# Seven block products in place of eight for the second MLP products of two chunks, with the sums of weight blocks made by accumulating DMAs

## The chip, the cores and the metric

The kernel runs on one core of a Trainium2 chip. The metric is the device time of one execution in microseconds. Three runs of the kernel before took 1099.1, 1102.78 and 1100.49 us; the median is 1100.49 us. The profile shows one further execution whose span, from the first to the last instruction, is 1099.7 us.

## The reference

One layer of a hybrid decoder for 512 prompt tokens and 32 new tokens (8 sequences of 4), which share all weights. Cut to the part that matters here:

```python
    y_m = h.astype(x.dtype) @ w_m_out                       # h: mLSTM output, gated
    merged = jax.nn.sigmoid(gc) * y_conv + jax.nn.sigmoid(gm) * y_m
    x1 = layer_norm(ALPHA * x + merged @ w_o, ln1_g, ln1_b)
    hid = jnp.square(jax.nn.relu(x1 @ w_ff1))               # 1024 -> 4096
    x2 = layer_norm(ALPHA * x1 + hid @ w_ff2, ln2_g, ln2_b) # 4096 -> 1024
```

Ahead of that stand the input projections (`w_in`), a short causal convolution of width 3 and the chunked mLSTM with its matrix states. Results are float32.

## The kernel before

**Layout.** All 544 tokens are held together, transposed: 8 tiles of 128 features (partitions) by 544 tokens, in large buffers called `slot0` to `slot7`. A half is 272 tokens; one half of one product fills part of one PSUM bank.

**One weight tile.** A weight tile is 1024 x 128 values, 512 KB, loaded by SyncE into one of three buffers `wr` (`wload`, L105) and split into two fp32r parts: `wh` by a cast on ScalarE (L140), `wl`, the remainder, by a subtract on VectorE (L141); each has three buffers too. Activations are kept as such pairs as well. A product is then `wh` by the high part, `wh` by the low part and `wl` by the high part, over 8 blocks of 128 input features and 2 halves of tokens: 48 matmuls of 272 columns per weight tile, all at L151 (`mm`, called by `mtile`).

**Order of the work.** Input projections with the prompt's mLSTM between them; the decode mLSTM, whose 32 states are read, updated and written back (L496 to L511; the write `out_cs_dram<-cr` is issued by GpSimd); convolution; `w_conv_out`, the gates and `w_m_out`; `w_o` and the first norm, half of the tokens by half; then the MLP in four chunks of 1024 hidden features (`for ck in range(4)`). A chunk is eight first-product tiles, each followed by relu, square and split (`act1`, L783 to L786), and eight second-product tiles, each added to `x1` by VectorE (L810, for the first chunk L807). The last chunk's second products go half by half with the last norm beside them. The instructions of the engines are put in order at build time by a scheduler that follows the program's dependencies and the buffers' reuse; each engine then runs its own list strictly in order.

**What the change touches.** Tiles 120 to 127 are the second products of chunk 1 and tiles 136 to 143 those of chunk 2; tiles 128 and 132 are the first two hidden tiles that chunk 2 now takes ahead. GpSimd issues no DMA and runs no instruction between 740 and 1040 us, SyncE only the weight loads.

Of the kernel before, what the change touches and what calls it, by code (L numbers as in the profile page):

```python
# [12 lines left out]
PSUM = bass.MemoryType.PSUM  # L13

# [17 lines left out]
# columns of the packed small operands  # L32
# [10 lines left out]
# order of the weight tiles  # L43
W_K, W_Q, W_O, W_V, W_CONV, W_YC, W_GC, W_GM, W_OUT, W_FF = 0, 8, 16, 24, 32, 56, 64, 72, 88, 96


@with_exitstack
def tile_hybrid(ctx: ExitStack, tc: tile.TileContext, xT, wt, wg, pk, caug,
# [118 lines left out]
    mstk = ExitStack()          # what the mLSTM keeps to its end  # L167
# [12 lines left out]
    pstk = ExitStack()          # what only the prompt's mLSTM needs  # L180
# [69 lines left out]
    # rows that matmuls spread over the partitions, in exact halves: c, w_inter of the prompt  # L250
# [31 lines left out]
    # per-token columns: a, w_inter, ws, exp(-m)  # L282
# [14 lines left out]
    # decay weights of S, transposed (s on partitions)  # L297
# [17 lines left out]
    qT, so = slot(3), slot(4)  # L315
# [9 lines left out]
    for ft in range(KT):  # L325
        h, d0 = ft // 2, (ft % 2) * P
        ps = mtile(W_V + ft, xh, xl)
        vt = tmp.tile([P, NT], F32, name=f"vt{ft}", tag="cg")
# [5 lines left out]
        vr = tmp.tile([P, 4, NS], F32, name=f"vr{ft}", tag="vr")  # L334
# [118 lines left out]
    # P: rows hi, hi, lo, lo, against v's rows hi, lo, hi, lo  # L453
# [7 lines left out]
    # k*ws: rows hi, hi, lo, lo of the 32 tokens  # L461
# [13 lines left out]
    # q*w_inter, hi and lo, each batch's columns alone  # L475
# [38 lines left out]
    finish(dp, nsb, NS, NC, 512)  # L514
    dstk.close()
    mstk.close()

# [1 line left out]
    bc = slot(5)  # L519
# [3 lines left out]
    NU = 2 + SEQ + DB * 6  # L523
    for ft in range(KT):
        ps = mtile(W_CONV + 3 * ft, xh, xl)
        cg = tmp.tile([P, NT], F32, name=f"cg{ft}", tag="cg")
        nc.scalar.copy(hview(cg), pv(ps))
        ps = mtile(W_CONV + 3 * ft + 1, xh, xl)
        ue = tmp.tile([P, NU], F32, name=f"ue{ft}", tag="ue")
# [22 lines left out]
    nc.sync.dma_start(conv_o, uco)

    def split(src, dh, dl, ft):
        nc.scalar.copy(r(dh[:, ft]), src)
        nc.vector.tensor_tensor(r(dl[:, ft]), src, dh[:, ft], op=ALU.subtract)

    bh, bl = slot(2), slot(3)
    split_ahead(W_YC, W_YC + 1)
    for ft in range(KT):  # L560
        split(bc[:, ft], bh, bl, ft)
    y1 = slot(5)
# [3 lines left out]
    for ft in range(KT):  # L566
        ps = mtile(W_GC + ft, xh, xl)
        sg = tmp.tile([P, NT], F32, name=f"sgc{ft}", tag="cg")
# [4 lines left out]
    late = pool("late")  # L573
    hh, hl = slot(6, late), slot(7, late)
    for ft in range(KT):
        split(so[:, ft], hh, hl, ft)
    mh, ml = slot(2), slot(3)
    for ft in range(KT):
        ps = mtile(W_GM + 2 * ft, xh, xl)
        sg = tmp.tile([P, NT], F32, name=f"sgm{ft}", tag="cg")  # L580
# [4 lines left out]
        split(sg, mh, ml, ft)  # L585

# [4 lines left out]
    x1 = slot(0)  # L591
    nc.sync.dma_start(x1, xT)
# [4 lines left out]
    lnp = pool("lnp", 2)  # L597

    def resident(i0, places, eng=nc.vector):
        out = [wsplit(i0 + j, eng) for j in range(3)]  # L600
        spots = []
        for j in range(3, KT):
            if not spots:
                n, pl = places.pop(0)
                t = pl.tile([P, KT * NT], F32R, name=f"res{i0}_{n}", tag=f"slot{n}")
                spots = [(t[:, 2 * g * KT * P:(2 * g + 1) * KT * P],
                          t[:, (2 * g + 1) * KT * P:(2 * g + 2) * KT * P]) for g in range(2)]
            hi, lo = spots.pop(0)
# [4 lines left out]
        return out  # L613

    def half(i, ft, w, ah, al, cs, mid=None):
# [4 lines left out]
    def lt(nm, tag, bufs=2, n=HN):  # L620
        return lnp.tile([P, HW], F32, name=nm, tag=tag, bufs=bufs)[:, :n]

# [6 lines left out]
    def rstd(nm, src):  # L629
        n = src.shape[1]  # L630
        rs = lt(nm, "lnr", n=n)
        nc.scalar.activation(rs, src, AF.Ln, bias=epst)
        nc.scalar.activation(rs, rs, AF.Exp, scale=-0.5)
        t = lt(nm + "n", "lnn", 1, n)         # a Newton step: y * (1.5 - 0.5 * (var + eps) * y * y)
# [5 lines left out]
    xh1, xl1 = slot(1), slot(5)  # L640

    def norm1a(hf, s):
# [3 lines left out]
        q = lt(f"aq{hf}", "lnq")  # L646
        for j in range(4):
            nc.vector.tensor_tensor(pair(x1, j, cs), pair(x1, j, cs), b2(pmn[:, :HN]),
                                    op=ALU.subtract)
            sq = lnp.tile([P, 2, HN], F32, name=f"asq{hf}{j}", tag="lnsq")  # L650
            nc.scalar.activation(sq, pair(x1, j, cs), AF.Square)
            if j > 0:
                nc.vector.tensor_tensor(sq, sq, sq0, op=ALU.add)
            sq0 = sq
        nc.vector.tensor_tensor(q, sq[:, 0], sq[:, 1], op=ALU.add)
        return q

    def norm1b(hf, q):
# [3 lines left out]
        rs = rstd(f"ar{hf}", pvr[:, :HN])  # L662
# [12 lines left out]
    res = resident(W_OUT, [(4, slots), (6, late), (7, late)])  # L675
    later = {}      # pieces of a norm, by the tile of the next half after which they come
# [5 lines left out]
    for hf in range(2):  # L682
        s1 = lt(f"as{hf}", "lns")
# [23 lines left out]
    def norm2_part(hf, ft, ps, st):  # L707
        """x = acc + ps, less the mean c of the first four tiles; sums of it and its squares"""
# [21 lines left out]
        for f in todo:  # L730
# [3 lines left out]
            sq = lt(f"bsq{hf}{f}", "lnsq2", n=n)  # L734
# [10 lines left out]
    def norm2(hf, st):  # L745
# [5 lines left out]
        m2 = lt(f"bm2{hf}", "lnm", n=n)  # L751
        nc.scalar.activation(m2, pmn[:, :n], AF.Square)
        nc.vector.tensor_tensor(m2, pq[:, :n], m2, op=ALU.subtract)
        rs = rstd(f"br{hf}", m2)
        ms = lt(f"bms{hf}", "lnm", n=n)
# [21 lines left out]
    for ck in range(4):  # L777
        dh, dl = (slot(2), slot(3)) if ck % 2 == 0 else (slot(6, late), slot(7, late))

        def act1(ft, src, cs, view):  # L780
            rl = tmp.tile([P, NT], F32, name=f"rl{ck}_{ft}_{cs.start}", tag="cg")
            rl_ = rl[:, :cs.stop - cs.start]
            nc.scalar.activation(view(rl_), src, AF.Relu)  # L783
            nc.vector.tensor_tensor(rl_, rl_, rl_, op=ALU.mult)  # L784
            nc.scalar.copy(r(dh[:, ft, cs]), rl_)  # L785
            nc.vector.tensor_tensor(r(dl[:, ft, cs]), rl_, dh[:, ft, cs], op=ALU.subtract)  # L786

        i0 = W_FF + 16 * ck
        if ck == 0:
            res = resident(i0, [(4, slots), (6, late), (7, late)], nc.gpsimd)  # L790
            for hf in range(2):
                for ft in range(KT):
                    run(ft)
                    act1(ft, half(i0 + ft, ft, res[ft], xh1, xl1, hv[hf]), hv[hf], lambda t: t)
        else:
            for ft in range(KT):
                act1(ft, pv(mtile(i0 + ft, xh1, xl1)), slice(0, NT), hview)
        if ck == 0:
            products_psum(2)
        if ck == 3:  # L800
            products_psum(4)
        if ck < 3:
            for ft in range(KT):
                ps = mtile(i0 + 8 + ft, dh, dl)
                a_ = hview(x1[:, ft])
                if ck == 0:
# [121 lines left out]
```

## Time and profile before

| What | Value |
|---|---|
| runs, median | 1099.1, 1102.78, 1100.49; 1100.49 us |
| span of the profiled execution | 1099.7 us |
| mean granted TensorE clock in it | 0.988 |
| busy: PE, VectorE, ScalarE, GpSimd | 97%, 49%, 32%, 13% of the span |
| HBM read, written | 97.32 MB, 11.81 MB |

The profile gives no time around the span of its execution; the median of the three runs stands 0.8 us above that span. PE is TensorE's matmul, PEld its weight load, which runs beside it; DVE is VectorE, ACT ScalarE, POOL GpSimd, SP SyncE. Matmuls are pipelined, so the duration of one (some 0.29 us) is longer than the distance from one to the next.

### The profile page before, as it was taken

How to read it: one execution, taken by the hardware profiler on the slowest of the kernel's cores; microseconds unless marked ns; L12 is line 12 of the kernel's file. 1: busy time of each engine (PE TensorE's matmuls, PEld its weight loads, DVE VectorE, ACT ScalarE, POOL GpSimd, SP SyncE). 2: the span in 40 equal slices, each digit the busy share in tenths (PEclk: the TensorE clock that was granted, in tenths of full speed). 3: DMA queues.
4: the chain of work that ended last, by engine and by line, in shares of the span. 5: the costliest groups of instructions: out<-in, count | busy, mean ns of one | idle time of the engine just before them, and what ended most of it. 6: DMA issues, size and time to landing. Idle time of an engine off the chain costs nothing.

```text
span 1099.7 us, 19420 instructions
## 1 busy us (share of the span) xinstructions
PE 1071.2 (97%) x8351; PEld 1060.0 (96%) x8351; DVE 535.5 (49%) x882; ACT 347.9 (32%) x516; POOL 143.0 (13%) x161
## 2 busy tenths in 40 slices
PE   8999999999999989999999999899999999999994
PEld 8999999999999989999999999899999999999994
DVE  5533223365578778522143359742344234334576
ACT  6431222232234334213222225441233133123432
POOL 1000230000017563003200004200000000000033
PEclk9999999999999999999999999899999999999997
DMA  6222222211136775222222342112222222222201
GB/s 233 98 78 77 97 83 90 77 45 53 40 135 203 241 209 162 95 96 77 97 79 95 123 171 96 58 58 75 80 97 77 97 81 93 94 80 97 96 23 60
DMA packets 34349, 110.37 MB, mean 100 GB/s; under 512 B 3928, under 2 KB 6232, under 8 KB 34008
## 3 DMA queue, kind: packets, MB, share of 16 engines
q1 hardware_dynamic: 31704, 100.69, 28.2%
q0 software_dynamic: 2560, 8.46, 2.0%
q8 instruction: 65, 1.06, 0.4%
q14 instruction: 20, 0.16, 0.1%
HBM read 97.32 MB, written 11.81 MB: 99 GB/s over the span
## 4 chain that ended last, share of the span: by engine, by line
PE 90%; DVE 4%; DMA 3%; ACT 1%; issue 1%; POOL 0%; SPq 0%; DVEq 0%; POOLq 0%; ACTq 0%
PE ps L151 82%; DMA cr<-in_caug_dram 1%; DMA out_cs_dram<-cr 1%; PE u L419 1%; PE pq L496 1%; PE n L405 1%; DVE slot L733 1%; PE S L386 1%; PE n L402 1%; DMA wr<-in_wt_dram 1%; DVE bq L743 1%; DVE slot L671 0%; PE us L507 0%; PE ht L367 0%; PE kt L412 0%
## 5 line engine op out<-in xcount | busy, mean ns | idle before, releaser
L151 PE MATMUL ps<-slot,wh 128*128 128x272 f32 (+1 forms) x4640 | 801.2, 290 | 3.9 <-DVE slot L671 1.8
L151 PEld LDWEIGHTS ps<-slot,wh 128*128 128x128 f32 x4640 | 669.0, 189 | 7.0 <-DVE slot L671 2.5
L151 PE MATMUL ps<-slot,wl 128*128 128x272 f32 (+1 forms) x2320 | 498.2, 289 | 0.0
L151 PEld LDWEIGHTS ps<-slot,wl 128*128 128x128 f32 x2320 | 371.6, 189 | 0.7
L140 ACT CAST wh<-wr 128x1024 fp32r<-128x1024 f32 x145 | 152.1, 1050 | 501.1 <-PE ps L151 437.3
L141 DVE TENSOR_TENSOR wl<-wr,wh 128x1024 fp32r<-128x1024 f32 x142 | 174.1, 1226 | 205.8 <-ACT wh L140 201.7
L151 PE MATMUL ps<-slot,res 128*128 128x272 f32 (+2 forms) x720 | 92.8, 289 | 0.0
L151 PEld LDWEIGHTS ps<-slot,res 128*128 128x128 f32 x720 | 91.3, 188 | 0.3
L726 POOL TENSOR_TENSOR slot<-slot,bc 128x288 f32<-128x288 f32 (+1 forms) x6 | 5.8, 992 | 360.2 <-ACT bc L724 360.2
L810 DVE TENSOR_TENSOR slot<-ps,slot 128x544 f32<-128x544 f32 x16 | 11.6, 725 | 59.3 <-PE ps L151 59.3
L503 POOL TENSOR_SCALAR km<-kk,pkt 128x256 fp32r<-128x256 f32 x32 | 37.3, 1168 | 14.6 <-PE us L507 7.8
L492 ACT CAST ch<-cr 128x516 fp32r<-128x516 f32 x32 | 19.9, 623 | 49.6 <-DMA cr<-in_caug_dram 28.7
L785 ACT CAST slot<-rl 128x544 fp32r<-128x544 f32 (+1 forms) x40 | 22.2, 556 | 37.2 <-DVE rl L784 37.1
L786 DVE TENSOR_TENSOR slot<-rl,slot 128x544 fp32r<-128x544 f32 (+1 forms) x40 | 24.4, 611 | 19.6 <-ACT slot L785 19.4
L509 DVE SCALAR_TENSOR_TENSOR cr<-cr,dec,us 128x258 f32<-128x258 f32 x64 | 29.3, 475 | 3.3 <-PE us L507 3.1
L324 POOL TENSOR_SCALAR slot<-slot,pkt 128x544 f32<-128x544 f32 x8 | 16.8, 2096 | 107.9 <-ACT slot L323 107.9
L493 DVE TENSOR_TENSOR cl<-cr,ch 128x516 fp32r<-128x516 f32 x32 | 22.1, 697 | 17.6 <-ACT ch L492 17.5
L784 DVE TENSOR_TENSOR rl<-rl 128x544 f32<-128x544 f32 (+1 forms) x40 | 24.3, 607 | 11.8 <-ACT rl L783 11.8
L570 POOL TENSOR_TENSOR slot<-slot,sgc 128x544 f32<-128x544 f32 x8 | 14.5, 1809 | 88.1 <-ACT sgc L569 88.1
L783 ACT ACTIVATE rl<-ps 128x544 f32<-128x544 f32 (+1 forms) x40 | 21.2, 529 | 14.3 <-PE ps L151 14.3
L496 PE MATMUL pq<-ch,qm 128*64 128x258 f32 x64 | 18.3, 292 | 5.9 <-ACT wh L140 3.2
L141 POOL TENSOR_TENSOR wl<-wr,wh 128x1024 fp32r<-128x1024 f32 x3 | 7.3, 2423 | 124.9 <-PE am L645 121.2
(258 smaller groups left out, 715.2 us busy)
## 6 DMA issues: line engine op xcount, KB each, us to landing
wr<-in_wt_dram SPq DMA_DIRECT2D x160, 512.0 KB, 3.5
cr<-in_caug_dram SPq DMA_DIRECT2D x32, 258.0 KB, 3.9
out_cs_dram<-cr POOLq DMA_DIRECT2D x32, 258.0 KB, 3.9
slot<-in_xT_dram SPq DMA_DIRECT2D x8, 272.0 KB, 6.3
slot<-in_xT_dram SPq DMA_DIRECT2D x1, 2176.0 KB, 8.5
out_yT_dram<-slot SPq DMA_DIRECT2D x4, 288.0 KB, 2.4
out_cp_dram<-state SPq DMA_DIRECT2D x1, 1028.0 KB
out_yT_dram<-slot SPq DMA_DIRECT2D x4, 256.0 KB, 2.3
```

Of the source, the lines that this page charges most:

```text
L140: nc.scalar.copy(hi, raw)
L141: eng.tensor_tensor(lo, raw, hi.bitcast(F32), op=ALU.subtract)
L151: nc.tensor.matmul(ps[:m, hf, :cs.stop - cs.start], w[:, ws], r(a[:, kt, cs]), start=(kt == 0 and w is wh and a is ah), stop=(kt == KT - 1 ...
L492: nc.scalar.copy(r(chh), cr)
L493: nc.vector.tensor_tensor(r(cl), cr, chh, op=ALU.subtract)
L496: nc.tensor.matmul(pq[:2 * NS, :VW], r(qm[:, dt, bb * 2 * NS:(bb + 1) * 2 * NS]), r(part[:, dt]), start=(bb == 0 and dt == 0 and part is chh),
L503: nc.gpsimd.tensor_scalar(r(km), kk[:, 2 * h:2 * h + 2].rearrange("p a d -> p (a d)"), col("bsel")[:, bb:bb + 1], None, op0=ALU.mult)
L509: nc.vector.scalar_tensor_tensor(cr[:, dt], cr[:, dt], dec[:, h, 4 + bb:5 + bb], pu[:, :VW], op0=ALU.mult, op1=ALU.add)
L783: nc.scalar.activation(view(rl_), src, AF.Relu)
L784: nc.vector.tensor_tensor(rl_, rl_, rl_, op=ALU.mult)
L785: nc.scalar.copy(r(dh[:, ft, cs]), rl_)
L786: nc.vector.tensor_tensor(r(dl[:, ft, cs]), rl_, dh[:, ft, cs], op=ALU.subtract)
```

## The change

**Second products of chunks 1 and 2.** A chunk's second product is a 1024 x 1024 weight block by 1024 hidden features of 544 tokens. It is taken as a 2 x 2 block product: the weight tiles in pairs `i0+j`, `i0+j+4` (their upper and lower 512 input features give `w11`, `w12`, `w21`, `w22`), the hidden features in two blocks and the tokens in two halves (`x11` to `x22`). Seven block products replace eight: W11, W12, S2, S1, S3, W22 and S4 by X11, X21, T2, T1, T3, T4 and X22. Each is 12 matmuls of 272 columns into one PSUM bank (`prod`); per pair that is 84 matmuls where two tiles had 96.

**Sums of weights.** `wpair` loads tile a and tile b (512 KB each) and `w21` into a 256 KB buffer `ws`, all from SyncE. GpSimd issues four DMAs that add a 256 KB block from HBM onto what lies in the buffer: `w22` onto b's upper half (S1), and onto `ws` first `w11` (S3), then `w22` (S2), then `w12` (S4). Each state of `ws` is cast and subtracted into its high and low part before the next block is added. `ws` has two buffers.

**Sums of operands.** `Opset` holds the high and low parts of X11, X21, X22 and of T1 to T4; T is made from each pair of hidden tiles by two subtractions on GpSimd and two on VectorE, each 272 wide. The signs are chosen such that partial results are only added or subtracted onto `x1` (`Added.onto`, eight evictions of 272 columns per pair). A bank that holds A goes on accumulating: A = W11, then + S2, + S3, + W22, and is read after each step.

**Hidden tiles.** `hidden(ck, j)` makes two hidden tiles; its square is on ScalarE over both tiles at once. The first two tiles of the next chunk are computed ahead of each stage of pairs.

**Elsewhere.** To make room, the mLSTM output is stored to HBM (`hD`, 2.2 MB) after the decode stage and read back before `w_m_out`; the convolution's result is split tile by tile in its loop; `x1` is loaded in eight DMAs; several tensors live in other buffers; the first norm takes its squares tile by tile; the first chunk's tiles use two single-bank PSUM tiles (`mtile1`). The first two additions of `w11` (for pairs 120 and 121) are issued right after the decode stage.

```diff
+    def wpair(i0, i1):
+        H = KH * P
+        a = wload(i0)
+        b = wp.tile([P, KT * P], F32, name=f"wr{i1}", tag="wr")
+        w11, w12, w21, w22 = (wt[i][:, k * H:(k + 1) * H] for i in (i0, i1) for k in range(2))
+        c = sp.tile([P, H], F32, name=f"ws{i0}", tag="ws", bufs=2)
+        def add(t, w):
+            nc.gpsimd.dma_start(t, w, accum_op=ALU.add)
+        nc.sync.dma_start(b, wt[i1])
+        nc.sync.dma_start(c, w21)
+        add(b[:, :H], w22)
+        add(c, w11)
+        gc = [pl.tile([P, KT * P], F32R, name=f"{k}{i0}c", tag=k) for k, pl in (("wh", wp), ("wl", wp))]
+        def half_(src, k):
+            hi, lo = (t[:, k * H:(k + 1) * H] for t in gc)
+            nc.scalar.copy(hi, src)
+            nc.vector.tensor_tensor(lo, src, hi.bitcast(F32), op=ALU.subtract)
+            return hi, lo
+        g1 = halves(f"{i0}a", a)
+        g2 = halves(f"{i0}b", b)
+        s3 = half_(c, 0)
+        add(c, w22)
+        s2 = half_(c, 1)
+        add(c, w12)
+        s4 = halves(f"{i0}d", c, "d")
...
+    def prod(ps, w, X, which, start):
+        wh, wl = w
+        for kt in range(KH):
+            ws = slice(kt * P, (kt + 1) * P)
+            for n, (w_, lo) in enumerate(((wh, 0), (wh, 1), (wl, 0))):
+                nc.tensor.matmul(ps[:, :HN], w_[:, ws], r(X.get(which, kt, lo)),
+                                 start=(start and kt == 0 and n == 0),
+                                 stop=(kt == KH - 1 and n == 2), skip_group_check=True)
...
+        prod(A, w["W11"], X, "X11", True)
+        ev.onto("c11", A[:, :HN])
+        step()
+        F = mmt(f"F{nm}")
+        prod(F, w["W12"], X, "X21", True)
+        ev.onto("c11", F[:, :HN])
+        step()
+        prod(A, w["S2"], X, "T2", False)
+        ev.onto("c12", A[:, :HN])
+        D = mmt(f"D{nm}")
+        prod(D, w["S1"], X, "T1", True)
+        prod(A, w["S3"], X, "T3", False)
+        ev.onto("c22", A[:, :HN])
+        ev.onto("c22", D[:, :HN])
+        def t0():
+            prod(A, w["W22"], X, "T4", False)
+            ev.onto("c21", A[:, :HN])
+        def t1():
+            prod(D, w["S4"], X, "X22", False)
+            ev.onto("c12", D[:, :HN])
+        tail.extend((t0, t1))
...
-        if ck < 3:
-            for ft in range(KT):
-                ps = mtile(i0 + 8 + ft, dh, dl)
...
-                    nc.vector.tensor_tensor(a_, pv(ps), a_, op=ALU.add)
...
+    for ck in (1, 2):
...
+        ahead_()
+        for j in range(1, KH):
+            hidden(ck, j)()
+        ahead_ = hidden(ck + 1, 0)
+        for j in range(KH):
+            i0 = W_FF + 16 * ck + 8
+            spair(i0 + j, i0 + j + KH, D[ck], Added(prows(x1, j)))
+        flush()
```

TensorE before, from the end of tile 120 to the start of 121 (each row stands for two matmuls, one per half of the tokens, in two banks):

```order
L151 MATMUL ps120_8794<-slot6_8306,wh120_8790 128x272 x2
L151 MATMUL ps120_8794<-slot7_8307,wh120_8790 128x272 x2
L151 MATMUL ps120_8794<-slot6_8306,wl120_8791 128x272 x2
L151 MATMUL ps121_8850<-slot6_8306,wh121_8846 128x272 x2
L151 MATMUL ps121_8850<-slot7_8307,wh121_8846 128x272 x2
```

Tile 121 goes on in other banks, and tile 120's banks are read meanwhile.

TensorE now, in pair 120 (the tiles 120 and 124), from the end of S3 (`wh120c`, `wl120c`) to the start of W22 (`wh120b`):

```order
L671 MATMUL A120_9009<-slot2_8463,wh120c_8989 128x272
L671 MATMUL A120_9009<-slot3_8464,wh120c_8989 128x272
L671 MATMUL A120_9009<-slot2_8463,wl120c_8990 128x272
L671 MATMUL A120_9009<-slot2_8463,wh120b_8995 128x272
L671 MATMUL A120_9009<-slot3_8464,wh120b_8995 128x272
```

S3 and W22 go into the same bank A120, one right behind the other, with a read of A120 by VectorE between them.

GpSimd now, in the pairs of chunk 1 (`wr126` and `wr127` are the b tiles of pairs 122 and 123; the `ws` rows with x2 are the additions of `w22` and then `w12`, a single `ws` row is that of `w11` or, for `ws120`, one of the others):

```order
L641 DMA ws120_8984<-in_wt_dram 128x512
L563 TENSOR_TENSOR ttd2_0_9477<-hid2_0_8863 128x272
L564 TENSOR_TENSOR ttd2_0_9477<-hid2_0_8863 128x272
L641 DMA ws120_8984<-in_wt_dram 128x512
L641 DMA wr126_9201<-in_wt_dram 128x512
L641 DMA ws122_9202<-in_wt_dram 128x512
L641 DMA ws121_9080<-in_wt_dram 128x512 x2
L641 DMA wr127_9323<-in_wt_dram 128x512
L641 DMA ws123_9324<-in_wt_dram 128x512
L641 DMA ws122_9202<-in_wt_dram 128x512 x2
L641 DMA ws136_9992<-in_wt_dram 128x512
L641 DMA ws123_9324<-in_wt_dram 128x512 x2
```

Pair 121's additions of `w22` and `w12` stand behind pair 122's addition of `w11`, and so on for each pair that follows. Before, this engine had no row here.

SyncE now, the loads at the same place (`wr` of 1024 columns is a plain load of a tile, `ws` of 512 the load of `w21`):

```order
L127 DMA wr122_9199<-in_wt_dram 128x1024
L643 DMA wr126_9201<-in_wt_dram 128x1024
L127 DMA wr123_9321<-in_wt_dram 128x1024
L644 DMA ws122_9202<-in_wt_dram 128x512
L643 DMA wr127_9323<-in_wt_dram 128x1024
L127 DMA wr129_9485<-in_wt_dram 128x1024
L644 DMA ws123_9324<-in_wt_dram 128x512
```

The load of `ws122` stands behind that of `wr123`; it also waits until the last state of `ws120`, whose buffer it takes, has been split.

## Rows read from the trace of the kernel before

**Rows 1.** The page's first part: busy time, share of the span, instructions.

```profile
span 1099.7 us, 19420 instructions
PE 1071.2 (97%) x8351; PEld 1060.0 (96%) x8351; DVE 535.5 (49%) x882; ACT 347.9 (32%) x516; POOL 143.0 (13%) x161
```

**Rows 2.** The chain of work that ended last, by engine.

```profile
PE 90%; DVE 4%; DMA 3%; ACT 1%; issue 1%; POOL 0%; SPq 0%; DVEq 0%; POOLq 0%; ACTq 0%
```

**Rows 3.** Windows: us; busy PE, PEld, DVE, ACT, POOL; clock; DMA share; GB/s.

```profile
343.00:428.00 85.00, 79.14 (x621) 78.09 (x620) 65.05 (x137) 31.65 (x48) 49.55 (x64) 0.98 0.72 223
672.00:706.00 34.00, 29.72 (x204) 28.30 (x203) 29.71 (x40) 16.67 (x31) 13.69 (x6) 0.90 0.27 93
740.00:1040.00 300.00, 299.45 (x2385) 299.24 (x2384) 115.75 (x128) 84.20 (x103) 0.00 (x0) 1.00 0.27 89
750.00:800.00 50.00, 50.00 (x401) 50.00 (x401) 16.22 (x17) 9.56 (x10) 0.00 (x0) 1.00 0.29 95
```

**Rows 4.** Groups in 740 to 1040 us: count, busy, mean ns, idle before.

```profile
L151 PE MATMUL ps<-slot,wh 128*128 128x272 f32 x1536 | 255.0, 288 | 0.5 <-ACT rl L783 0.5
...
L141 DVE TENSOR_TENSOR wl<-wr,wh 128x1024 fp32r<-128x1024 f32 x48 | 58.8, 1226 | 68.2 <-ACT wh L140 65.7
L140 ACT CAST wh<-wr 128x1024 fp32r<-128x1024 f32 x48 | 50.4, 1050 | 174.4 <-PE ps L151 174.4
L786 DVE TENSOR_TENSOR slot<-rl,slot 128x544 fp32r<-128x544 f32 x24 | 17.4, 726 | 16.5 <-ACT slot L785 16.5
...
L785 ACT CAST slot<-rl 128x544 fp32r<-128x544 f32 x24 | 15.5, 647 | 33.2 <-DVE rl L784 33.2
...
L810 DVE TENSOR_TENSOR slot<-ps,slot 128x544 f32<-128x544 f32 x16 | 11.6, 725 | 59.3 <-PE ps L151 59.3
...
L786 DVE TENSOR_TENSOR slot<-rl,slot 128x272 fp32r<-128x272 f32 x1 | 0.4, 444 | 0.5 <-ACT slot L785 0.5
```

**Rows 5.** DMA issues: count, KB each, median us from issue to landing.

```profile
wr<-in_wt_dram SPq DMA_DIRECT2D x160, 512.0 KB, 3.5
...
out_cs_dram<-cr POOLq DMA_DIRECT2D x32, 258.0 KB, 3.9
...
slot<-in_xT_dram SPq DMA_DIRECT2D x1, 2176.0 KB, 8.5
...
out_yT_dram<-slot SPq DMA_DIRECT2D x4, 256.0 KB, 2.3
wgr<-in_wg_dram SPq DMA_DIRECT2D x1, 256.0 KB, 2.6
```

**Rows 6.** The stores GpSimd issues, alone: ns of one issue; us to landing.

```profile
L511 POOL DMA_DIRECT2D out_cs_dram<-cr x32: 539/600/749, 335.4 to 429.1; - x32
...
DMA to landing us min/median/max: 2.5/3.9/6.8
```

**Rows 7.** Timeline in the first norm: start, duration, instruction, idle before it.

```profile
682.70 0.29 PE L151 MATMUL ps<-slot,wh 128*128 128x272 f32 x1
683.14 0.42 DVE L689 SCALAR_TENSOR_TENSOR slot<-slot,ps 128x272 f32<-128x272 f32 x1
...
683.62 0.39 PE L151 MATMUL ps<-slot,wh 128*128 128x272 f32 x1 [0.63 <-DVE slot L689]
```

More of the change, by code (lines that the diff above doesn't have):

```diff
@@ L23 @@
 KT = 8
+KH = KT // 2
 NH = 4
@@ L613, in resident, with rplaces @@
         return out
+    def rplaces(t):
+        return sum((spots(slot(k, (P, KT * NT), F32R)) for k in (0, 1)), []) + ppspot(t)
     def half(i, ft, w, ah, al, cs, mid=None):
@@ L618, in half, with __init__, __call__ @@
         return ps[:, 0, :cs.stop - cs.start]
-    def lt(nm, tag, bufs=2, n=HN):
-        return lnp.tile([P, HW], F32, name=nm, tag=tag, bufs=bufs)[:, :n]
+    class Small:
+        def __init__(self, tiles):
+            self.free = [t[:, i] for t in tiles for i in range(t.shape[1])]
+            self.of, self.n = {}, {}
+        def __call__(self, tag, bufs=2, n=None):
+            if tag not in self.of:
+                self.of[tag] = [self.free.pop(0) for _ in range(bufs)]
+            k = self.n[tag] = self.n.get(tag, -1) + 1
+            t = self.of[tag][k % bufs]
+            return t if n is None else t[:, :n]
     def pair(t, j, cs):
@@ L638, in rstd @@
         return rs
-    xh1, xl1 = slot(1), slot(5)
+    lt1 = Small([ztile(f"ln{k}").rearrange("p a (b n) -> p (a b) n", b=2) for k in range(3)])
     def norm1a(hf, s):
@@ L649, in norm1a @@
                                     op=ALU.subtract)
[L650 to L655, printed above, removed]
+            for i in range(2):
+                sq = sqs[2 * (j % 2) + i]
+                nc.scalar.activation(sq, x1[:, 2 * j + i, cs], AF.Square)
+                if 2 * j + i > 0:
+                    nc.vector.tensor_tensor(q, sq, q if 2 * j + i > 1 else sqs[0], op=ALU.add)
         return q
@@ L775, in norm2 @@
             nc.sync.dma_start(yT[:, 2 * j:2 * j + 2, cs], pair(x1, j, cs))
[L777 to L786, printed above, removed]
+    D = {}
@@ L788, in tile_hybrid, with hidden @@
+    def hidden(ck, j):
         i0 = W_FF + 16 * ck
-        if ck == 0:
-            res = resident(i0, [(4, slots), (6, late), (7, late)], nc.gpsimd)
+        z = ztile(f"hid{ck}_{j}")
+        for a in range(2):
+            ps = mtile1(i0 + j + KH * a, xh1, xl1)
             for hf in range(2):
-                for ft in range(KT):
-                    run(ft)
-                    act1(ft, half(i0 + ft, ft, res[ft], xh1, xl1, hv[hf]), hv[hf], lambda t: t)
-        else:
-            for ft in range(KT):
-                act1(ft, pv(mtile(i0 + ft, xh1, xl1)), slice(0, NT), hview)
@@ new lines, in hidden, with put, mtile1 @@
+                nc.scalar.activation(z[:, a, hv[hf]], ps[hf], AF.Relu)
+        nc.scalar.activation(z, z, AF.Square)
+        def put():
+            if ck < 3:
+                D[ck].take(f"d{ck}_{j}", j, z, nc.gpsimd)
+            else:
+                split(prows(dh, j), prows(dl, j), z)
+        return put
+    def mtile1(i, ah, al):
+        wh, wl = wsplit(i)
+        pss = [mmt(f"ps{i}_{hf}")[:, :HN] for hf in range(2)]
+        for kt in range(KT):
+            ws = slice(kt * P, (kt + 1) * P)
+            for n, (w, a) in enumerate(((wh, ah), (wh, al), (wl, ah))):
+                for hf, cs in enumerate(hv):
+                    nc.tensor.matmul(pss[hf], w[:, ws], r(a[:, kt, cs]),
+                                     start=(kt == 0 and n == 0), stop=(kt == KT - 1 and n == 2))
+        return pss
@@ new lines, in tile_hybrid @@
+    res = resident(W_FF, rplaces(pp), nc.gpsimd)
+    dh, dl = slot(2), slot(3)
+    for hf in range(2):
+        for ft in range(KT):
+            run(ft)
+            ps = half(W_FF + ft, ft, res[ft], xh1, xl1, hv[hf])
+            rl = sp.tile([P, 2, NT], F32, name=f"rl{ft}_{hf}", tag="zb")[:, 0, :HN]
+            nc.scalar.activation(rl, ps, AF.Relu)
+            nc.vector.tensor_tensor(rl, rl, rl, op=ALU.mult)
+            split(dh[:, ft, hv[hf]], dl[:, ft, hv[hf]], rl)
+    ahead_ = hidden(1, 0)
@@ new lines, in tile_hybrid, with sums @@
+    dh, dl = slot(2), slot(3)
+    ahead_()
+    for j in range(1, KH):
+        hidden(3, j)()
+    i0 = W_FF + 56
+    lt2 = Small([o2.tile([P, 15, HW], F32, name="ln2", tag="tl")])
+    res = resident(i0, rplaces(o2.tile([P, 2 * KH * 3 * HN], F32, name="pp2", tag="pp")))
+    for hf in range(2):
+        st = {}
+        def sums(hf=hf, st=st):
+            st["ps"] = aux(f"bm{hf}"), aux(f"bv{hf}")
+            for ps, t0 in zip(st["ps"], (st["s"], st["q"])):
+                nc.tensor.matmul(ps[:, :hv2[hf].stop - hv2[hf].start], onek, t0,
+                                 start=True, stop=False)
+        for ft in range(KT):
+            run(ft)
+            ps = half(i0 + ft, ft, res[ft], dh, dl, hv2[hf], sums if ft == 7 else None)
+            with tc.high_priority(offset=300):
+                norm2_part(lt2, hf, ft, ps, st)
+        if hf == 0:
+            later[1] = lambda st=st: norm2(lt2, 0, st)
+        else:
+            norm2(lt2, 1, st)
```

221 lines of the change are left out of this document (140 added, 81 removed).

## The prediction

> **What bounds the kernel now.** I read the page's busy times first: TensorE is busy 97% of the span and no other engine reaches half [rows 1]. The chain of waits says the same: 90% of the path to the end is PE [rows 2]. Then I took windows over the stages, because an average hides stalls. From 740 to 1040 us, where nearly all of the MLP runs, PE works without a break: 2385 matmuls in 300.0 us, 0.126 us each, and 401 in 50.0 us (0.125) at the full clock [rows 3]. There the only wait listed before the 1536 matmuls on `wh` is 0.5 us in all [rows 4]. VectorE is busy 116 us of these 300, ScalarE 84, GpSimd none, DMA 27%. So here a matmul removed is worth 0.125 us if nothing else comes late, and an engine other than PE has room. The decode stage (343 to 428) and the first norm (672 to 706) are where PE waits now, 5.9 and 4.3 us [rows 3].
>
> **What is removed.** Two chunks of 8 x 48 matmuls become 4 x 84 each: 768 - 672 = 96 matmuls fewer, 96 x 0.125 = 12.0 us. Per pair of tiles that is 12.0 us before and 10.5 us after. Everything else is a question of whether PE gets its operands and banks in time at this shorter pace.
>
> **What PE waits for in each pair, even with instant DMAs.** Three places follow from the order. (1) S3 and W22 go into the same bank with VectorE's read between them. The timeline of the first norm has such a place: the last matmul starts at 682.70 and lasts 0.29, the 0.42 us read follows, the next matmul starts at 683.62, idle 0.63 [rows 7]. Measured from start to start this is 0.92 less one pace of 0.125, 0.80; with back-to-back handing (0.29 + 0.43 + 0.06 - 0.125) it is 0.65. I take 0.7. (2) The a tile of the next pair is cast only when W22's products with `wh` are done, because its buffer is that of W22's tile or later in ScalarE's list. Cast and subtract take 1.05 + 1.23 [rows 4]; between stand the 12 matmuls of S4 (1.5 us), and the third matmul of W11 needs the low part: 2.28 + 0.1 - 1.5 - 0.25 gives about 0.65. (3) The same for the b tile's low part before S1, again about 0.65. Sum 2.0 us per pair. So the pair runs at 12.5 us, not 10.5, and is slower than the 12.0 of before. Bounds: none of it, if the waits are hidden by the order (10.5), or 0.8 + 0.75 + 0.75 (12.8).
>
> **The chain of the weight sums.** One `ws` buffer per pair goes through: S2's cast done, subtract (512 columns; the 544-wide row has 726 ns [rows 4], so 0.68), addition of `w12` lands (A), cast (544 wide 647 ns [rows 4], so 0.6), subtract (0.68) and 0.1 of signals, then the buffer is free two pairs on: plain load of `w21` lands (L), GpSimd issues the addition of `w11` (0.6, the median issue [rows 6]), addition of `w22` lands (A), cast (0.65). Two buffers would let two such chains overlap, but GpSimd's list does not: the addition of `w22` for pair j+1 stands behind the addition of `w11` for pair j+2, which waits for the load into the buffer that pair j has just left. Hence one pair's period is 2A + L + 0.6 + 2.75.
>
> L is a plain load of 256 KB: 2.6 us in `wgr`, 2.3 in the `out_yT` stores, 3.5 for the 512 KB tiles [rows 5]; behind a 512 KB load in the same list I take 3.0. For A no row exists. The nearest are GpSimd's stores of 258 KB: 2.5, 3.9 and 6.8 us as least, median and most, issue included [rows 6], those in a stage where DMA is busy 72% against 27% here [rows 3]. An addition moves as much and reads its destination too, which speaks for more; the quieter queues speak for less. I take the median, 3.9, and keep 2.5 and 6.8 as ends.
>
> The Trainium skill, "DMA: Bandwidth & Descriptors", section "Anatomy of one DMA — SWDGE (gpsimd) path", gives 2.0 us plus bytes over 436e3 for a DMA from GpSimd, an estimate of 2.6 us for 256 KB. The stores of before touch that only at their least, 2.5, and stand at 3.9 in the middle [rows 6]; by the page's figure this sum would come out as in the second case below. The same page's "Rules for kernel authors" says that an accumulating DMA reads its destination and writes it later, with nothing that holds the bytes between; so the additions to one buffer have to be waited for one after another, as the order shows they are. No run here has such a DMA yet.
>
> With A 3.9 and L 3.0 the period is 14.15 us. Let 0 be the end of the two hidden tiles ahead of chunk 1's pairs. Pair 120's S2 is ready at about 2 + A = 5.9, where PE comes to it at 5.0: 0.9 lost. S2 of pair 121 has 143 matmuls ahead of it in PE's list (17.9 us), the three waits (2.0) and that 0.9: 20.8; the chain alone would have it ready at 5.9 + 14.15 = 20.05, which delays nothing. Two more periods bring the last pair's S2 to 49.1. Behind it are 46 matmuls and one read (about 6.3 us), and 23 matmuls that belong to the next stage (about 3.1 with a wait) have been done ahead: the stage ends at 52.3. Before, it is 8 x 48 x 0.125 = 48.0: +4.3. In chunk 2 no further `w11` stands in front of the last pair: +3.7. Together +8.0.
>
> **The rest.** Splits: the a and b tiles and three states of `ws` take ScalarE 1.05 x 2 + 0.6 x 3 = 3.9 us per pair, and VectorE 1.23 x 2 + 0.68 x 3 with eight evictions of 0.43 takes 7.9 us, hidden while they come in time. The operand sums (four 272-wide per tile pair, 0.44 [rows 4]) are off PE's path behind the hidden tiles. The store of the mLSTM output (2.2 MB; a load of that size landed in 8.5 us [rows 5]) stands in SyncE's list before weight loads that are three tiles, 18 us, ahead; hidden, if not 0 to 2 us. Splitting the convolution's result in its loop takes away a wait of about 1.5 us after decode, while decode has by the order 36 to 39 fewer product matmuls to fill its gaps: 0 to 4.5 us, of which I count 2. Sum +1, bounds -4 and +5.
>
> **Sum.** 1099.7 + 8.0 + 1 = 1108.7 for the profiled execution; the median of the runs stands 0.8 above the span: 1109.5.
>
> **The rivals.**
> 1. Additions land in 2.5 to 3.2 us. With 2.6 the period of the chain (11.5) is below the 12.5 of the PE waits: S2 of pair 121 is at 19.9, the last at 19.9 + 25.1 = 45.0 and the stage ends at 48.2, +0.2 twice; with the rest about 1102. Range 1098 to 1104: no change. For it: quiet queues, and the least rows. Against: the median row, and the extra read.
> 2. Faster: the three waits in each pair are covered (by reads that start as soon as the bank's last matmul is through, splits that run earlier than I derive) and additions are quick. Then the 12.0 us come off in full: 1089; with half of the waits, 8 x 1.0, 1097. It decides if a pair takes under 12.0 us. For it: VectorE and ScalarE have room. Against: the same-bank read is in PE's order whatever the splits do.
> 3. Additions are slow, A from 4.5 to 6.8. At 5.0 the period is 16.35, S2 of pair 121 moves to 23.35 and the stage ends at 59.25: +11.3 and +10.5, 1123; at 6.0, 66.3: +18 and +17.5, 1137. For it: reading and writing the destination, and two additions of one pair back to back on the same engines. Against: DMA busy only 27%.
>
> **How the numbers follow.** The forecast case has A from 3.3 (period 12.95, +2.5) to 4.5 (+14.7): 1104 to 1117, chance 0.47. No change 0.21, faster 0.13, slow additions 0.19. About 0.3%, 3.3 us, is what a measurement here can tell from no change. Faster by more is rival 2 without its upper end and a lucky rest, 0.13; within it is rival 1 with the edges of its neighbours, 0.20; slower is the rest, 0.67. The range 1093 to 1131 holds the forecast case, rival 1, the upper end of rival 2 and the slow additions up to 5.5 us.
>
> **What would show it.** In the windows of the pairs 84 matmuls per pair, some 14 us from pair to pair, and PE waiting for ScalarE's cast and VectorE's subtract of the `c` tiles (S2) for 1.5 to 2 us in each, on top of three waits of 0.6 to 0.8. The casts of `ws` in turn wait for the additions; their median landing tells A directly. GpSimd's queue waits for the plain load of `ws`. Wrong would be: PE's clock falling in these stages, pairs at 10.5 to 11 us, additions landing in under 3 us, or a loss in the decode stage or at the read-back of the mLSTM output that is larger than that of the pairs.

## The result: 43.6 us slower

Six runs of the changed kernel took 1138.3 to 1146.04 us, median 1143.6, against 1100.0 us for the kernel before in the same comparison: ratio 1.0394, interval 1.0374 to 1.0414. The forecast was 1109.5 us with a range of 1093 to 1131. The sign held, and so did the place of the loss; its size was outside the range. The page of the changed kernel begins, beside [rows 1]:

```profile
span 1144.3 us, 19568 instructions
## 1 busy us (share of the span) xinstructions
PE 1076.7 (94%) x8255; PEld 1059.2 (93%) x8255; DVE 563.2 (49%) x952; ACT 382.5 (33%) x584; POOL 183.1 (16%) x209
```

The 96 matmuls are gone (8351 to 8255), and PE is nevertheless busy 5.5 us longer: some of its matmuls run slower. Windows over the two stages of pairs show where (columns as in [rows 3]; the pairs of chunk 1 are 852 to 925, those of chunk 2 967.9 to 1044):

```profile
852.00:925.00 73.00, 56.24 (x379) 53.40 (x378) 29.66 (x48) 18.85 (x26) 13.62 (x16) 0.91 0.53 120
967.90:1044.00 76.10, 59.36 (x420) 56.95 (x419) 30.94 (x50) 20.90 (x28) 10.45 (x12) 0.91 0.48 113
```

In the first pair stage 379 matmuls at 0.125 us would be 47.3 us. They took 73.0: PE stood still for 73.0 - 56.2 = 16.8 us and was busy for 56.2 - 47.3 = 8.9 us more than that. In the second, 420 matmuls are 52.4 us of 76.1: 16.7 of waits and 7.0 of longer work. Most of the longer work is the lower clock (0.91 on average): by the starts in the trace some 60 matmuls of the first stage and some 40 of the second follow one another in 0.225 in place of 0.125 us, about 6 and 4 us. Much of the rest is the end of the last matmul before each wait, whose full 0.29 us count as busy. Together 49.4 us lost, less the 12.0 of removed matmuls: +37.4 of the 44.6 us between the two spans. What PE waited for, by line (us in all, times, longest), beside the 0.5 us of [rows 4]:

```profile
PE A L671 <- ACT wh137c L651: 5.3, 1, 5.3
...
PE A L671 <- ACT wh138c L651: 4.7, 1, 4.7
PE A L671 <- ACT wh123c L651: 4.6, 1, 4.6
PE ps L173 <- ACT cg L586: 3.6, 1, 3.6
PE A L671 <- DVE x L726: 3.6, 6, 0.9
...
PE A L671 <- ACT wh122c L651: 3.0, 1, 3.0
PE A L671 <- ACT wh121c L651: 2.8, 1, 2.8
```

The waits for a `c` tile, 20.4 us in these five, are S2's cast in five of the eight pairs; these are the rows that the forecast named, at 1.5 to 2 us each. The chain of waits over chunk 1 tells what the cast waited for; of its pieces from pair 121's S2 to pair 122's (start, duration, what):

```profile
869.92 6.44 DMA ws<-in_wt_dram
...
876.40 1.61 issue
...
878.02 3.78 DMA ws<-in_wt_dram
...
881.82 0.63 ACT wh121d L627
...
882.47 0.70 DVE wl121d L628
...
883.19 2.97 DMA ws<-in_wt_dram
...
886.72 0.53 POOL ws L641
887.25 7.14 DMA ws<-in_wt_dram
```

Read downward: pair 121's `w22` lands at 876.4; cast and subtract (the 1.61, issue of GpSimd's DMA pending on them); `w12` lands in 3.78; cast, subtract; the buffer is free and `w21` of pair 123 loads in 2.97; GpSimd issues `w11` for it; and only then `w22` for pair 122, which takes 7.14. That is 18.0 us from 876.38 to 894.41, and no matmul is in it. GpSimd's own timeline shows the two additions leave as one block (x2) at 869.38 and 886.71. An issue is listed with 0.87 us, where the stores of before had 0.6 [rows 6], but the next one starts 0.53 us behind it, as the chain above shows:

```profile
869.38 1.76 POOL L641 DMA_DIRECT2D ws<-in_wt_dram  x2 [6.44 <-DMA ws<-in_wt_dram]
878.02 0.87 POOL L641 DMA_DIRECT2D ws<-in_wt_dram  x1 [6.88 <-DVE wl121c L652]
878.55 1.22 POOL L641 DMA_DIRECT2D wr<-in_wt_dram  x1
886.71 1.75 POOL L641 DMA_DIRECT2D ws<-in_wt_dram  x2 [6.94 <-DVE wl122c L652]
```

And the lower clock follows the wait. TensorE's timeline around it:

```profile
873.80 0.41 PE L671 MATMUL F<-slot,wh122a 128*128 128x272 f32 x2
877.05 0.82 PE L671 MATMUL A<-slot,wh121c 128*128 128x272 f32 x2 [2.83 <-ACT wh121c L651]
877.67 0.43 PE L671 MATMUL F<-slot,wl122a 128*128 128x272 f32 x1
877.89 0.47 PE L671 MATMUL A<-slot,wl121c 128*128 128x272 f32 x1
```

Before the 2.83 us of idleness a matmul follows the other in 0.125 us, after it in 0.225. The windows after the wait and behind it (the clock stands before the last two numbers):

```profile
877.00:882.70 5.70, 5.65 (x24) 5.65 (x25) 3.29 (x6) 1.56 (x2) 1.76 (x2) 0.50 0.52 79
883.00:894.00 11.00, 8.03 (x60) 7.37 (x59) 3.65 (x7) 1.67 (x2) 1.75 (x2) 1.00 0.67 165
```

0.50 is the lower of the two levels, 1.2 GHz; in this part of the kernel before, the mean granted clock was 1.00 [rows 3].

### The profile page after: what moved, and what is told of

The parts are those of the page before. It is cut to its first block, busy times and chain, and to the rows that moved or that the text cites. A ratio compares the mean times of both kernels' runs of the same rounds, so it can differ in the third digit from the quotient of the medians.

```text
span 1144.3 us, 19568 instructions
## 1 busy us (share of the span) xinstructions
PE 1076.7 (94%) x8255; PEld 1059.2 (93%) x8255; DVE 563.2 (49%) x952; ACT 382.5 (33%) x584; POOL 183.1 (16%) x209
## 4 chain that ended last, share of the span: by engine, by line
PE 76%; DMA 13%; DVE 6%; issue 3%; ACT 2%; POOL 0%; SPq 0%; POOLq 0%; DVEq 0%; ACTq 0%
PE ps L173 53%; PE ps L995 15%; DMA ws<-in_wt_dram 9%; DMA wr<-in_wt_dram 1%; DMA cr<-in_caug_dram 1%; PE u L442 1%; DMA out_cs_dram<-cr 1%; PE pq L519 1%; PE n L428 1%; DVE x L921 1%; DVE x L856 1%; PE S L409 1%; PE n L425 1%; PE A L671 1%; DMA out_cp_dram<-state 1%
## 5 line engine op out<-in xcount | busy, mean ns | idle before, releaser
L173 PE MATMUL ps<-slot,wh 128*128 128x272 f32 (+2 forms) x2752 | 485.6, 292 | 8.0 <-ACT cg L586 3.6
L173 PEld LDWEIGHTS ps<-slot,wh 128*128 128x128 f32 x2752 | 401.0, 190 | 10.7 <-ACT cg L586 3.9
L173 PE MATMUL ps<-slot,wl 128*128 128x272 f32 (+2 forms) x1376 | 298.6, 291 | 0.0
L173 PEld LDWEIGHTS ps<-slot,wl 128*128 128x128 f32 x1376 | 221.9, 190 | 0.8 <-DVE wl L163 0.2
L995 PE MATMUL ps<-xh,wh 128*128 128x272 f32 x384 | 83.8, 289 | 0.0
L995 PE MATMUL ps<-xh,wl 128*128 128x272 f32 x384 | 82.7, 289 | 1.1 <-DVE wl L163 1.1
L995 PE MATMUL ps<-pp,wh 128*128 128x272 f32 x384 | 83.2, 288 | 0.0
L995 PEld LDWEIGHTS ps<-xh,wl 128*128 128x128 f32 x384 | 61.2, 189 | 1.5 <-DVE wl L163 1.5
L995 PEld LDWEIGHTS ps<-xh,wh 128*128 128x128 f32 x384 | 62.3, 189 | 0.0
L995 PEld LDWEIGHTS ps<-pp,wh 128*128 128x128 f32 x384 | 62.1, 189 | 0.0
L641 POOL DMA_DIRECT2D ws<-in_wt_dram x24 | 21.0, 958 | 122.4 <-DMA ws<-in_wt_dram 27.6
L995 PEld LDWEIGHTS ps<-slot,wh 128*128 128x128 f32 x256 | 36.2, 188 | 0.0
L347 POOL TENSOR_SCALAR so<-so,pkt 128x544 f32<-128x544 f32 x8 | 16.7, 2092 | 108.0 <-ACT so L346 108.0
```

Source lines behind the costliest of these rows:

```text
L173: nc.tensor.matmul(ps[:m, hf, :cs.stop - cs.start], w[:, ws], r(a[:, kt, cs]), start=(kt == 0 and w is wh and a is ah), stop=(kt == KT - 1 ...
L347: nc.gpsimd.tensor_scalar(so[:, ft], so[:, ft], col("mhg")[:, ft:ft + 1], None, op0=ALU.mult)
L641: nc.gpsimd.dma_start(t, w, accum_op=ALU.add)
L995: nc.tensor.matmul(pss[hf], w[:, ws], r(a[:, kt, cs]), start=(kt == 0 and n == 0), stop=(kt == KT - 1 and n == 2))
```

## Experiments

Theory: GpSimd's list ties each pair's S2 to the buffer of the pair before, and the second of two additions that leave together is slow. Rivals: additions are slow wherever they stand; or the rest of the rearrangement carries the loss. Ratios are to the kernel before, run beside each.

| Kernel | us, median | ratio, interval |
|---|---|---|
| changed kernel | 1143.6 | 1.0394, 1.0374 to 1.0414 |
| eight products in its layout | 1103.28 | 1.0032, 1.0016 to 1.0047 |
| eight `ws` buffers | 1111.98 | 1.0102, 1.0073 to 1.0131 |
| four `ws` buffers | 1131.36 | one run |
| plain DMAs for the additions | 1116.02 | one run |
| additions of half the columns | 1122.5 | one run |
| only `w11` plain | 1138.58 | one run |
| sums on GpSimd | 1099.57 | 1.0014, 0.9992 to 1.0036 |
| sums on GpSimd, own `c` buffers | 1092.85 | 0.9947, 0.9929 to 0.9965 |
| sums on VectorE, own `c` buffers | 1092.65 | 0.9951, 0.9933 to 0.9969 |
| six `ws` buffers, own `c` buffers | 1109.92 | 1.0108, 1.0073 to 1.0144 |

**Eight products in the new layout.**

```diff
-            spair(i0 + j, i0 + j + KH, D[ck], Added(prows(x1, j)))
+            ps = mtile1(W_FF + 16 * ck + 8 + ft, dh, dl)
+            for hf in range(2):
+                nc.vector.tensor_tensor(a_, ps[hf], a_, op=ALU.add)
```

> The changed kernel with the second products of chunks 1 and 2 made as eight ordinary products again (two single-bank tiles, 48 matmuls each, as its chunk 0 does); all other rearrangements stay (buffers, the mLSTM output through HBM, splits in the convolution loop, norm scratch). Theory: the pairs cost 37 us of the 44 and the rest of the rearrangement 7 (5 us of products that wait before 330 us, 4 in the last norm, 2 given back in the first norm): 1107, between 1104 and 1110. Rival, the pairs are all of it and the rest was pushed by them: 1100, within 2.

The rest costs 3.6 us, between the two expectations. The one wait that only the new layout has in the early stage is that for `cg` (3.6 us in the changed kernel, 3.3 here; none before).

**Eight, and four, `ws` buffers.**

```diff
-        c = sp.tile([P, H], F32, name=f"ws{i0}", tag="ws", bufs=2)
+        c = sp.tile([P, H], F32, name=f"ws{i0}", tag="ws", bufs=8)
```

> The changed kernel with eight ws buffers in place of two, one per pair: the loads of w21 and the additions of w11 all go ahead of the pairs, so no addition of w22 stands on GpSimd behind one that waits for a buffer. TensorE's order is the same as in the changed kernel. Theory: the chain through GpSimd's list is what delays S2; the waits for S2's cast fall from 22.5 us to under 3, a pair takes 12.5 to 13 us, additions that go out alone land in about 3.9 us and TensorE's clock stays full: about 1110. Rival, additions are slow in themselves (6 to 8 us for that of w22, whatever stands beside it): S2 is still late by some 1.7 us a pair, 1122 to 1130.

> The changed kernel with four ws buffers. By the order chunk 1 keeps the coupling (its additions of w22 still stand behind those of w11 for chunk 2's pairs, which wait for a buffer that a pair has just left), chunk 2 has none. Theory: chunk 1 stays at about 18 us per pair with S2 late by about 3, chunk 2 goes to 12.5 to 13: about 1127. Rival, slow additions or the waits of the order alone: both chunks alike.

With eight, 1111.98, as the theory had it: 31.6 us come back with the same additions and the same matmul order. S2 waits only for the first pair of each chunk (1.1 and 1.0 us). Each row below gives, behind the colon, the least, median and most duration of a pair's S2 and S3 matmuls on the high part, then the start of the first and of the last. The first is that of S2, and the distance of these starts from pair to pair is the pace; with eight buffers:

```profile
L671 PE MATMUL A<-slot,wh121c x16: 282/288/292, 872.2 to 877.3; 128*128 128x272 f32 x16
L671 PE MATMUL A<-slot,wh122c x16: 287/290/292, 885.1 to 890.3; 128*128 128x272 f32 x16
L671 PE MATMUL A<-slot,wh123c x16: 285/290/396, 898.0 to 905.4; 128*128 128x272 f32 x16
```

12.9 us per pair. With four, the coupling is in chunk 1 alone:

```profile
L671 PE MATMUL A<-slot,wh121c x16: 283/360/592, 876.0 to 881.9; 128*128 128x272 f32 x16
L671 PE MATMUL A<-slot,wh122c x16: 287/358/592, 894.6 to 901.4; 128*128 128x272 f32 x16
L671 PE MATMUL A<-slot,wh123c x16: 287/340/428, 912.4 to 921.3; 128*128 128x272 f32 x16
...
L671 PE MATMUL A<-slot,wh137c x16: 285/288/292, 988.6 to 993.8; 128*128 128x272 f32 x16
L671 PE MATMUL A<-slot,wh138c x16: 285/288/292, 1001.8 to 1007.0; 128*128 128x272 f32 x16
L671 PE MATMUL A<-slot,wh139c x16: 285/289/393, 1014.9 to 1022.3; 128*128 128x272 f32 x16
```

18 us per pair in chunk 1, 13.1 in chunk 2, in one execution with the same DMAs (1131.4 us, where about 1127 was expected). So the order decides; additions that are slow wherever they stand would slow both chunks. The next runs show that the order alone is not enough.

**What an addition costs.** Three kernels change only the DMAs: all four plain, all over half their columns, only `w11` plain. Each leaves some of the sums out, so its output is not the layer's and only its times are read.

```diff
-            nc.gpsimd.dma_start(t, w, accum_op=ALU.add)
+            nc.gpsimd.dma_start(t, w)                                       # plain
+            nc.gpsimd.dma_start(t[:, :H // 2], w[:, :H // 2], accum_op=ALU.add)  # half
-        add(c, w11)
+        nc.gpsimd.dma_start(c, w11)                                         # only w11 plain
```

> The changed kernel with the four additions per pair made plain DMAs of the same size on the same queue (the sums are left out: each overwrites). Theory: the order's coupling stays, so S2 stays late, but the second of two that go out together lands some 2 us earlier, since an addition holds the DMA engines for 1.67 us against 0.69 for a plain store (from the queue's share of time): a pair 16 us in place of 18, about 1130. Rival, the accumulation itself is the whole cost: landings of 2.5 to 3 us, S2 hardly late, under 1116.

> The changed kernel with additions over only the first 256 of their 512 columns (the rest of the sums is left out). GpSimd's coupling stays; by the order two of the pairs' S2 stand a few matmuls earlier. Theory: an addition holds the DMA engines in proportion to its bytes, so one alone lands in about 3.0 in place of 3.8 us and the second of two in 4.5 to 5 in place of 7; a pair about 14, total 1118 to 1122. Rival, the cost is per DMA (the issue, a read-modify round trip) and hardly falls: 7 us stay 6 or more, over 1132.

> The changed kernel with only the addition of w11 made a plain DMA (w21 is left out of the sums). The order's coupling is unchanged, but the first of the two DMAs that go out together no longer reads its destination. Theory: the second waits for the engines' time of the first, 0.8 in place of 1.7 us; it lands about 1 us earlier (6.5 in place of 7.5) and the total is 1134 to 1139. Rival, two accumulations disturb each other beyond that (each waits for the other's read and write): the second lands in 5 us or less, total under 1126.

In each chain of waits stands a `w12` that leaves alone and a `w22` that leaves second. All plain:

```profile
872.82 2.84 DMA ws<-in_wt_dram
...
880.76 4.50 DMA ws<-in_wt_dram
```

Half the columns:

```profile
872.53 3.01 DMA ws<-in_wt_dram
...
881.49 4.43 DMA ws<-in_wt_dram
```

Only `w11` plain:

```profile
878.75 3.91 DMA ws<-in_wt_dram
...
889.32 5.12 DMA ws<-in_wt_dram
```

The run with plain DMAs took 1116.0 us, where I had expected 1130. It lies at the edge of the rival (under 1116): with the order kept, one run gives back 27.6 of the 31.6 us that eight buffers give back, and the longest waits for S2's cast are 1.4, 0.9 and 0.6 us. I had cut the second landing by 2 us, but the five `w22` that leave second landed in 3.4 to 5.0 us, and the lone ones in 2.8 to 3.7, some 1 us less than lone additions. So the loss needs both: an order that puts every landing of the weight sums into one chain, and additions that land late in it. Taking away either one gives most of it back.

In the changed kernel the five `w22` that leave second land in 6.4 to 8.2 us (7.5 on average), lone additions in 4.2 on average; behind a plain `w11` they land in 4.2 to 6.2 (5.1). So 2.4 of the 3.3 us by which the second is later go when the first no longer adds. The queue's share of time says how long the engines are held: 6.6% of 16 engines for all software DMAs, 4.3% with the additions plain, 2.0% without any of them. Over the span and 32 additions that is 1.67 us of each engine per addition and 0.81 per plain DMA.

Half the columns took 1122.5 us, 0.5 above its theory's range and far from the rival's 1132: lone ones landed in about 3.0, the second ones in 3.6 to 6.3. The `w11` run is in the range of the one theory by its total (1138.6) and at the edge of the other by its landings. Its total hides a part: from the S3 cast of pair 120 to the S2 cast of pair 139 it took 166.5 us (854.58 to 1021.09), the changed kernel 175.6 (852.07 to 1027.72), 9.1 less, and the stages ahead were 2.5 us longer in its one execution. That an addition costs more than its engine time when another stands before it is shown; by which mechanism is open. No run keeps the chain and sends the two additions apart.

**Sums on GpSimd, without and with buffers for the `c` tile; sums on VectorE; DMA sums with `c` buffers.**

```diff
-        add(b[:, :H], w22)
-        add(c, w11)
+        nc.gpsimd.tensor_tensor(c3, w21, w11, op=ALU.add)   # w.. are now the loaded tiles
+        nc.gpsimd.tensor_tensor(w21, w21, w22, op=ALU.add)
+        nc.gpsimd.tensor_tensor(c2, c3, w22, op=ALU.add)
+        nc.gpsimd.tensor_tensor(c4, c2, w12, op=ALU.add)
...
-        gc = [pl.tile([P, KT * P], F32R, name=f"{k}{i0}c", tag=k) for k, pl in (("wh", wp), ("wl", wp))]
+        gc = [sp.tile([P, KT * P], F32R, name=f"{k}{i0}c", tag=k + "c") for k in ("wh", "wl")]
```

> The changed kernel with the weight sums made by four GpSimd additions of 512 columns per pair from the two loaded tiles, each sum in a buffer of its own; no accumulating DMA, no load of w21. By the order S3 and W22 no longer stand next to each other in one bank. Theory: with the sums early, PE waits only for the low parts of the a and b tiles (0.5 us each); a pair takes about 11.3 us in place of 18, S2 is never waited for: about 1098 (1103.3 of the eight-product version less 8 x 0.7). Rival, the seven products are no gain even with quick sums, since splits and evictions on VectorE set the pace: a pair 12.9 us as with eight ws buffers, 1110 or more.

> As the version with GpSimd sums, and the tile of S3 and S2 has buffers of its own, so the three wh and wl buffers hold a and b tiles alone. Theory: the splits of a and b start a tile earlier and their waits go; a pair takes 10.6 to 11 us, total 1092 to 1096, faster than the kernel before. Rival, VectorE or GpSimd is late instead: 1100 or more.

> As the fastest version so far (sums from the loaded tiles, own buffers), with the four additions per pair on VectorE in place of GpSimd. Theory: VectorE's subtracts no longer stretch from 0.69 to 1.4 to 1.8 us beside GpSimd's additions, but VectorE has 10.7 us of work in a pair of 10.5, so evictions come late: 1094 to 1100, no faster than with GpSimd. Rival, the stretching was the larger cost: 1088 to 1091.

> The changed kernel, sums still by accumulating DMAs, with six ws buffers and with buffers of its own for the tile of S3 and S2 (the scratch of the first chunk's relu is made smaller for room). By the order no addition of w22 stands behind one that has to wait long, and W22 still follows S3 in one bank. Theory: the waits of the order for the low parts of a and b go, the same-bank wait of 0.8 us a pair stays; a pair takes 11.3 us against 12.9 with eight ws buffers alone: 1097, between 1094 and 1101. Rival, the additions' own landing (4.2 us each, three in a row) becomes the pace at this shorter pair: 1105 or more.

The first came out as expected (1099.57). The second, 1092.85, beats both kernels: with early sums no S3 stands beside W22 in one bank, and with `c` buffers apart PE waits for nothing in the pairs. The VectorE version is equal to it, 1092.65, with no wait of PE listed from 835 to 1000 us; both of its expectations were off by little. In it an addition is 0.69 us:

```profile
L643 DVE TENSOR_TENSOR ws<-ws,wr 128x512 f32<-128x512 f32 x8 | 5.5, 688 | 0.1
```

on GpSimd, in the second version, up to three times that:

```profile
L642 POOL TENSOR_TENSOR ws<-ws,wr 128x512 f32<-128x512 f32 x8 | 17.2, 2151 | 0.0
```

The last missed: 1109.92 against 1097. Its number is the rival's (1105 or more). My reading of its order was wrong: one addition of `w11`, for pair 139, still stands ahead of pair 122's `w22` and waits for a buffer. In its profile (an execution of 1105.57 us, the shortest of four) that one place costs PE 4.7 us of waiting; the rival's own mechanism, S2 late in the other pairs, shows with 1.1 and 0.8 us there. The 4.4 us by which the median is longer than this execution were not taken apart. The two longest waits of the pairs:

```profile
PE A L671 <- ACT wh122c L651: 4.7, 1, 4.7
PE A L671 <- DVE x L726: 4.1, 4, 2.5
```

## Why the prediction was right in kind and wrong in size

**What bounds the kernel; what is removed.** Right in the main: 96 matmuls at 0.125 us. By the ratios to the kernel before, each run beside it, the two versions with early sums lie 0.85% and 0.81% below the eight products in the same layout (0.9947 and 0.9951 against 1.0032), some 9 of the 12.0 us. Where the other 3 go was not looked for.

**Waits in each pair with instant DMAs.** The three places are there. Same bank: 866.46 to 867.28 from matmul to matmul, 0.69 over the pace, 0.7 forecast. Low parts: 0.53 and 0.74 idle, which from matmul to matmul is 0.69 and 0.90 over the pace, 0.65 each forecast. Their sum was a little too small: 12.9 us per pair with eight buffers, not 12.5, and the first and last pairs of a chunk lose more. With the chain out of the way this part of the change costs 8.7 us net of the matmuls (1111.98 less 1103.28), where rival 1, which has these waits alone, had 0.4.

**The chain of the weight sums.** This is the step that failed, in one term. "Hence one pair's period is 2A + L + 0.6 + 2.75" put the same A, 3.9, for both additions.

| Term | forecast | measured, 876.38 to 894.41 |
|---|---|---|
| `w12`, alone | 3.9 | 3.78 |
| `w22`, behind `w11` | 3.9 | 7.14 |
| load of `w21` | 3.0 | 2.97 |
| landing of `w21` to issue of `w22` | 0.6 | 1.1 |
| casts, subtracts, signals | 2.75 | 3.04 |
| period | 14.15 | 18.03 |

S2 was forecast at 5.9, 20.8, 35.0 and 49.1 us of the stage; its casts start at 5.7, 24.3, 42.3 and 61.2 (857.75, 876.38, 894.41 and 913.26 less 852.07). The order had said that `w22` of one pair goes out right behind `w11` of the next, on the same queue. I had noted it as a thing to be waited for and not as a thing that makes `w22` itself land late. The case "additions are slow" named it ("two additions of one pair back to back", though by the order the two belong to neighbouring pairs) and put 0.19 on A as a whole, from 4.5 up. Over the five coupled periods `w12` took 4.25 us on average and `w22` 7.50, 5.9 in the mean; with that its own rule gives some 1136, and the range had held slow additions only up to 5.5.

Most of the miss of 34 us is this term. Chunk 1's last S2 came 12.1 us later than forecast, and its three `w22` behind a `w11` (6.44, 7.14 and 8.13 us for 3.9) are 10.0 of them. Chunk 2's came at 59.6 (1027.72 less 968.12) for some 48.5, 11.1 later, and its two (8.22 and 7.59) are 8.0 of them. Behind the last S2 each chunk lost about 3 us more than forecast: the last `w12` (4.73 and 4.22 us) and its split stand in the chain there. The rest of the rearrangement cost 2.6 more. In the 1.1 of the table the issue of `w11` is 0.53, as forecast; the other 0.5, between the landing of the load and that issue, was not in the sum.

**The clock.** Left out of the sum; named under what would make it wrong. It fell after each of the five long waits. By the chain of waits this cost nothing by itself in the pairs: from the end of the hidden tiles until after the last S2 no matmul stands in that chain, so a faster PE would only have waited longer, and the 10 us of slower matmuls counted above lie beside it. The two pieces of PE that stand on either side in chunk 1 (in chunk 2 the chain is without PE from 968.10 to 1035.43):

```profile
851.91 0.14 PE ps L995
...
921.47 1.78 PE A L671 x12
```

No run holds the clock up to test this.

**A lone DMA from GpSimd.** The plain DMAs that left alone took 2.8 to 3.7 us, the additions alone 3.8 and more. The Trainium skill, "DMA: Bandwidth & Descriptors", "Anatomy of one DMA — SWDGE (gpsimd) path", gives an estimate of 2.6 us for 256 KB. The least of the plain ones come close to it, no addition does.

**The rest.** +1 forecast with bounds of -4 and +5; 3.6 measured, in the bounds. Of its parts the wait for `cg` was not foreseen.

**The rivals.** Quick additions (rivals 1 and 2): excluded by the landings, of which none is under 3.7 us, and by the measured time. Slow additions (rival 3): the nearest, in one of the two additions of a period and only behind another. The forecast that chunk 2's last pair is not held up is right: its `w22` left alone and landed in 3.97 us.

## What to carry to other kernels

When DMAs that depend on buffers share one in-order queue, write down for each what stands ahead of it and what that one waits for: here the queue tied each pair to the buffer of the pair before, although there were two, and one buffer per pair gave 31.6 us back. What stands in such a chain sets its cost: plain DMAs in the same order gave back 27.6. Price a DMA by its place, alone or behind another, and not by one median. If the operands of a sum are on the chip already, try adding them there: here, with buffers of their own for the split sums, that made the seven products 0.5% faster than the kernel before.

## What the hardware showed unexpectedly

An accumulating DMA of 256 KB holds each DMA engine about twice as long as a plain one (1.67 against 0.81 us). Its issue is listed with 0.87 us in place of 0.54, though the next one starts 0.54 us behind either. Of two in a row the second lands in 7.5 us on average, where one alone lands in 4.2. With eight buffers one that left 1.51 us behind another (874.01 after 872.50) still took 7.04 us; in the changed kernel one that left 2.69 us behind (862.08 after 859.38) took 3.99.

VectorE and GpSimd slow each other when both read two tensors from SBUF. With the sums on GpSimd (the version without own `c` buffers) a 512-column subtract on VectorE that runs beside them takes 1.4 to 1.8 us, 0.69 alone (at 875.75), and a 512-column sum on GpSimd 1.6 to 2.3 us, 1.3 alone (at 877.90); both timelines, VectorE first:

```profile
866.45 2.19 DVE L628 TENSOR_TENSOR wl121b<-wr,wh121b 128x1024 fp32r<-128x1024 f32 x1 [0.56 <-ACT wh121b L627]
...
868.91 3.12 DVE L649 TENSOR_TENSOR wl121c<-ws,wh121c 128x512 fp32r<-128x512 f32 x2
```

```profile
867.64 2.15 POOL L641 TENSOR_TENSOR wr<-wr 128x512 f32<-128x512 f32 x1
869.74 1.74 POOL L642 TENSOR_TENSOR ws<-ws,wr 128x512 f32<-128x512 f32 x1
871.56 1.61 POOL L643 TENSOR_TENSOR ws<-ws,wr 128x512 f32<-128x512 f32 x1
```

The Trainium skill, "SBUF — State Buffer", "Who interferes with whom", says that a VectorE instruction with two SBUF inputs contends with a GpSimd instruction that reads SBUF; these rows agree.
